# Four reorderings in a hybrid encoder block: scan products in three rows a chunk, the last convolution taps behind the gating, a block split behind a copy, part loads behind residual tiles

## The chip, the core and the metric

The kernel runs on one core of one Trainium2 chip. The core's engines run beside each other, each with a queue of its own that it works off in order: TensorE (PE in the profile) multiplies matrices, VectorE (DVE), ScalarE (ACT) and GpSimd (POOL) work elementwise, and SyncE (SP) issues the DMAs. Semaphores tie the queues together. The metric is the device time of one launch in microseconds; of several runs the median is taken.

## The reference

One layer over 1024 tokens of width 1024, everything in float32:

```python
h = rms_norm(x, mix_norm_g)
p = h @ w_in                                   # split into the inputs of three groups
y_a = spatial_gating(gelu(gm_u), gelu(gm_v))   # layer norm, causal 128x128 blocks, 4 heads
y_b = silu(layer_norm(depthwise_conv31(cv_a * sigmoid(cv_g)) + b))
y_c = gated_deltanet(dn_q, dn_k, dn_v, ...)    # chunked scan, 4 heads of 128
x = x + concat(y_a, y_b, y_c) @ w_out
h = rms_norm(x, ffn_norm_g)
x = x + (silu(h @ w_gate) * (h @ w_up)) @ w_down
return rms_norm(x, final_norm_g)
```

## The kernel before

Activations lie transposed, 128 features on the partitions by tokens; the 1024 tokens are two halves of 512 (`hf` 0 and 1). A float32 operand of a large product is split into a high part, cast on ACT (name ending in `_h`), and the remainder, subtracted on DVE (`_l`); each product of two operands is three matmuls, high by high, high by low, low by high. All matmuls of 128x512 go through PE in an order that a scheduling layer writes down while the kernel is built: it records all operations, models each engine as a queue and lets the first ready operation of the program's order go ahead, so a statement's place in the code, its data and explicit `tc.issue_after(...)` constraints decide where the instruction lands. Pools with few buffers (50 tiles `d`, 4 PSUM tiles `mm`, 3 `aux`, 2 raw weight buffers) make an operation wait for the one that frees its tile.

The stages around the change, in order of time:

- **Scan (245 to 350 us; lines 487 to 600).** The gated delta rule in 8 chunks of 128 tokens. `prep(c)` (L487) inverts a triangular matrix per head by blocks of 32 and 64: `pw` (L504) 8 products of 32x32, `pm` and `pmt` (L509, L515) 4 and 8 of 32x32, `pw2` (L519) and `pm2` (L524) 4 each of 64x64, with small copies on ACT and DVE between. The loop then does per chunk `ks` (L554, keys by state `Sn`), DVE's `vsr` (L556), `u` (L560), `S` (L567) with DVE's state `Sn` (L573), `os` (L580), `o` (L585), four 128x128 products each. Between them PE works on projection matmuls `pv` (L635) and `pg` (L258).
- **Gating and convolution.** `gating()` multiplies `sp` (L656) into `ugr` on DVE (L658). The depthwise convolution is 31 taps for each of 2 channel tiles `j` and 2 halves `hf`, all on DVE, 128x512 each (L692, L694): 120 instructions on L694.
- **Output projection (373 to 478 us; L757).** `mix_conv(0)` calls `conv_out(0)`: transposes `cvt` of the convolved first half (L704), statistics on DVE (L708, L709), normalization `ytk` on DVE (L714), transposes `cvb` back (L719), SiLU and a cast on ACT (`ybt`, then `myb_h`), the remainder on DVE (`myb_l`). Output tiles `po` of the first half are begun three at a time: 16 products each from `ya` and `yc`, then six from `myb`.
- **FFN (478 to 905 us).** Gate and up projections by a 7-product block scheme: blocks `B11`, `T1` to `T4`, `B22` of the activations, weights `w1` to `w7` of each `Matrix`. The products of a matrix accumulate in `X`; after the seventh, `product7` (L897), ACT copies `X` to `c22` (L900), and only then may PE add the fourth (`w4` by `T4`, L909). The block `T4` is made by subtractions on DVE (L1012), casts on ACT and remainders on DVE (`T_h`, `T_l`).
- **Down projection (905 us to the end).** `Down` objects `d00` to `d16` (group, output tile), in two groups of inputs. Each adds its products to residual tiles that come from HBM: `acc` (L1060) loads a tile `xad` from `X1d`, `add` (L1072) adds the product on DVE, `put` stores it. `product7` of a `Down` loads two tiles and adds `X` to the first, and PE's next product into `X` waits for that. `Group.load` (L1120) fetches the blocks (`T1f1`, `T2f1`, `T4f1`, ... of group 1) from HBM, four 256 KB DMAs each; weights `d_r` come as 512 KB DMAs (L137). All loads and stores stand in SP's one queue.

Of the kernel before, what the change touches and what calls it, by code (L numbers as in the profile page):

```python
# [38 lines left out]
def tile_kernel(ctx: ExitStack, tc: tile.TileContext, xT, wt, wub, wv, wout, wg, wu, wd, wdl,  # L39
# [447 lines left out]
    def prep(c):  # L487
        hf, i = divmod(c, NH)
        cs = slice(i * P, (i + 1) * P)
        M, MT, lt = d3(f"M{c}"), d3(f"MT{c}"), d3(f"ltr{c}")  # L490
        nc.sync.dma_start(M, Md[:, c * NH:(c + 1) * NH])
        nc.sync.dma_start(lt, LTd[:, c * NH:(c + 1) * NH])
        qk, vs, kd = d3(f"qkr{c}"), d3(f"vsr{c}"), d3(f"kd{c}")
        nc.sync.dma_start(vs, VSd[c])
        nc.sync.dma_start(kd, KTd[c])
        prep.loaded.append(nc.sync.dma_start(qk, QKd[c]).ins)
        DVE.transpose(MT.rearrange("p a b -> p (a b)"), M.rearrange("p a b -> p (a b)"))

        lo, up = (slice(0, 32), slice(64, 96)), (slice(32, 64), slice(96, 128))
        pw = aux3(f"pw{c}")  # L500
        for h in range(NH):
            for j, k in zip(lo, up):
                PE.matmul(pw[k, h, 0:32], lhsT=lt[j, h, k], rhs=M[j, h, j], start=True, stop=True)
        W = sp.tile([P, NH, 64], F32, tag="W", name="W")[:, :, 0:32]  # L504
        for k in up:
            ACT.copy(W[k], pw[k, :, 0:32])
        pm = aux3(f"pm{c}")
# [4 lines left out]
        for h in range(NH):
            for j, k in zip(lo, up):
                PE.matmul(pm[j, h, 0:32], lhsT=W[k, h], rhs=MT[k, h, k], start=True, stop=True)
        for j, k in zip(lo, up):  # L515
            DVE.tensor_scalar(MT[j, :, k], pm[j, :, 0:32], -1.0, None, op0=ALU.mult)
        pw = aux3(f"pw2{c}")
# [890 lines left out]
```

## Time and profile before

| | us |
|---|---|
| Median of three runs (1148.93 to 1153.93) | 1151.78 |
| The profiled execution | 1150.55 |
| Its span, first to last instruction | 1148.8 |
| PE busy in it | 1130.3 |
| DVE, ACT, POOL busy | 798.0, 479.1, 225.5 |
| Longest wait of PE for one operation | 3.0 |

PE works for 98% of the span; what the other engines do costs time only where PE stands still for it, or where the clock that is granted to it falls.

### The profile page before, as it was taken

The page shows a single profiled execution, that of the slowest core. Times are in us where ns is not written, and L with a number is a line of the kernel's source. Part 1 is how long each engine was busy: PE and PEld are TensorE (multiplying, and loading weights), DVE is VectorE, ACT ScalarE, POOL GpSimd, SP SyncE. Part 2 cuts the span into 40 slices and gives each one's busy share as a digit, 9 for nine tenths or more (in the row PEclk, how much of TensorE's full clock was granted, in tenths as well). Part 3 has the DMA queues.
Part 4 walks back from the last instruction along what each step waited for, and adds up shares of the span by engine and source line. Part 5 has one row for each costly group of instructions (what it writes and reads, how often), then busy time and mean ns, then how long its engine had stood idle before and what let it go on. Part 6 is the DMA issues. An engine that isn't in the chain of part 4 may idle for free.

```text
span 1148.8 us, 15996 instructions
## 1 busy us (share of the span) xinstructions
PE 1130.3 (98%) x5878; PEld 934.7 (81%) x5878; DVE 798.0 (69%) x1297; ACT 479.1 (42%) x1006; POOL 225.5 (20%) x192
## 2 busy tenths in 40 slices
PE   9999999999999999989999999999999999899997
PEld 7889888889788888877888888888888877688897
DVE  6799879868889757696654655565544786685623
ACT  7456561224435654453333333333334533432522
POOL 0000230011213221205432323323232000000142
PEclk9999999999999999999999999999999999999999
DMA  7134342463423454314332322232234778778312
GB/s 241 57 118 167 111 138 102 123 208 112 131 65 109 147 182 167 129 37 140 136 110 83 129 92 101 92 129 92 100 129 151 247 243 280 249 266 277 146 70 78
DMA packets 87325, 163.17 MB, mean 142 GB/s; under 512 B 16432, under 2 KB 28368, under 8 KB 87248
## 3 DMA queue, kind: packets, MB, share of 16 engines
q1 hardware_dynamic: 87248, 162.16, 42.0%
q8 instruction: 46, 0.75, 0.3%
q14 instruction: 31, 0.25, 0.1%
HBM read 115.45 MB, written 46.68 MB: 141 GB/s over the span
## 4 chain that ended last, share of the span: by engine, by line
PE 66%; DVE 4%; DMA 2%; issue 1%; SPq 0%; POOL 0%; ACT 0%; POOLq 0%; ACTq 0%; DVEq 0%
PE Xu L836 10%; PE Xg L836 10%; PE po L757 8%; PE Xd L836 7%; PE pdl L1158 5%; PE Zu L836 5%; PE Zg L836 5%; PE pg L258 3%; PE Zd L836 3%; PE Yu L836 2%; PE Yg L836 2%; PE Yd L836 2%; DMA d_r<-in_wd_dram 1%; PE Wu L836 0%; DVE T_l L90 0%
## 5 line engine op out<-in xcount | busy, mean ns | idle before, releaser
L694 DVE SCALAR_TENSOR_TENSOR ca<-cy,vec,ca 128x512 f32<-128x512 f32 x120 | 92.6, 794 | 0.5
L1342 POOL TENSOR_TENSOR sqf<-sqf,sqt 128x256 f32<-128x256 f32 (+1 forms) x19 | 17.9, 940 | 228.3 <-ACT sqt L1340 228.1
L131 DVE TENSOR_TENSOR wo_l<-wo_r,wo_h 128x512 fp32r<-128x512 f32 x32 | 26.6, 843 | 20.0 <-ACT wo_h L130 20.0
L901 DVE TENSOR_TENSOR c22u<-Zu,c22u 128x512 f32<-128x512 f32 x11 | 7.6, 692 | 45.0 <-ACT c22u L900 45.0
L1074 DVE TENSOR_TENSOR xad<-Xd,xad 128x512 f32<-128x512 f32 x32 | 21.8, 688 | 24.1 <-PE Xd L836 14.2
L885 POOL TENSOR_TENSOR s2u<-u_r,s2u 128x512 f32<-128x512 f32 x11 | 19.7, 1787 | 85.8 <-DVE w6u_l L131 85.8
L819 POOL TENSOR_TENSOR sqa<-sqa,xr 128x512 f32<-128x512 f32 x13 | 17.7, 1362 | 71.1 <-ACT xr L817 45.2
L1158 PE MATMUL pdl<-ff_h,wd_h 128*128 128x256 f32 (+1 forms) x96 | 30.9, 322 | 0.0
L1158 PE MATMUL pdl<-ff_h,wd_l 128*128 128x256 f32 (+1 forms) x96 | 30.6, 319 | 0.0
L1158 PE MATMUL pdl<-ff_l,wd_h 128*128 128x256 f32 (+1 forms) x96 | 30.5, 318 | 0.0
L885 POOL TENSOR_TENSOR s2g<-g_r,s2g 128x512 f32<-128x512 f32 x11 | 18.1, 1642 | 62.6 <-DVE w6g_l L131 62.6
L870 POOL TENSOR_TENSOR s1g<-g_r 128x512 f32<-128x512 f32 x11 | 14.2, 1293 | 76.3 <-DMA g_r<-in_wg_dram 76.3
L836 PE MATMUL Yu<-b,w2u_h 128*128 128x512 f32 x88 | 27.9, 396 | 0.0
L836 PE MATMUL Xu<-b,w1u_h 128*128 128x512 f32 x88 | 27.6, 395 | 0.0
L836 PE MATMUL Xg<-b,w1g_h 128*128 128x512 f32 x88 | 27.5, 394 | 0.0
L836 PE MATMUL Yg<-b,w2g_h 128*128 128x512 f32 x88 | 27.5, 393 | 0.0
L1333 DVE TENSOR_TENSOR xf<-pdl,xf 128x256 f32<-128x256 f32 (+1 forms) x18 | 9.2, 514 | 25.9 <-PE pdl L1158 25.8
L130 ACT CAST wo_h<-wo_r 128x512 fp32r<-128x512 f32 x32 | 19.6, 618 | 18.0 <-PE po L757 14.7
L870 POOL TENSOR_TENSOR s1u<-u_r 128x512 f32<-128x512 f32 x10 | 14.6, 1455 | 62.3 <-DMA u_r<-in_wu_dram 57.2
L131 DVE TENSOR_TENSOR w2g_l<-g_r,w2g_h 128x512 fp32r<-128x512 f32 x11 | 16.2, 1476 | 15.0 <-ACT w2g_h L130 15.0
L900 ACT COPY c22u<-Xu 128x512 f32<-128x512 f32 x11 | 6.5, 587 | 47.8 <-PE Xu L836 47.8
L900 ACT COPY c22g<-Xg 128x512 f32<-128x512 f32 x11 | 6.4, 586 | 46.8 <-PE Xg L836 46.8
(580 smaller groups left out, 3869.9 us busy)
## 6 DMA issues: line engine op xcount, KB each, us to landing
u_r<-in_wu_dram SPq DMA_DIRECT2D x24, 512.0 KB, 3.9
g_r<-in_wg_dram SPq DMA_DIRECT2D x24, 512.0 KB, 3.8
d_r<-in_wd_dram SPq DMA_DIRECT2D x24, 512.0 KB, 5.0
wo_r<-in_wout_dram SPq DMA_DIRECT2D x16, 512.0 KB, 4.1
xad<-X1d SPq DMA_DIRECT2D x32, 256.0 KB, 5.0
X1d<-xad SPq DMA_DIRECT2D x28, 256.0 KB, 3.3
FFd<-T SPq DMA_DIRECT2D x24, 256.0 KB, 2.0
xr<-in_xT_dram SPq DMA_DIRECT2D x16, 256.0 KB, 3.7
```

The source lines that it names most:

```text
L130: ACT.copy(hi, raw)
L131: DVE.tensor_tensor(lo, raw, f32(hi), op=ALU.subtract)
L258: proj.last = PE.matmul(ps[hf], lhsT=cols(wtile, a, kt * P), rhs=(xh, xl)[b][kt][hf], start=(kt == 0 and a + b == 0), stop=(kt == KT - 1 a ...
L694: DVE.scalar_tensor_tensor(o, y(m), w(m), o, op0=ALU.mult, op1=ALU.add)
L757: out_mm.last = PE.matmul(ps, lhsT=cols(wtile, a, kt * P), rhs=mix[hf][kt][b], start=(kt == 0 and a + b == 0), stop=(kt == 3 and a == 1))
L819: POOL.tensor_tensor(acc, acc, xr, op=ALU.add)
L836: ins = PE.matmul(ps, lhsT=w[a][:, k * P:(k + 1) * P], rhs=blk[b][k], start=(first and k == 0 and a + b == 0), stop=(last and k == HB - 1 ...
L870: eng.tensor_tensor(self.s1, a21, a22, op=ALU.add)
L885: (eng or POOL).tensor_tensor(self.s2, self.part(0, 1), self.s2, op=ALU.subtract)
L1074: self.added = DVE.tensor_tensor(x, ps, x, op=ALU.add).ins
L1158: PE.matmul(ps[:, 0:cs.stop - cs.start], lhsT=cols(wtile, a, c), rhs=ff[f, hf][b][:, cs], start=(first and i + a + b == 0), stop=(last and ...
L1342: POOL.tensor_tensor(acc[:, 0:w], acc[:, 0:w], t[:, 0:w], op=ALU.add)
```

## The change

1. `prep` becomes a class `Prep` with four steps. `pm` and `pmt` write one PSUM tile and stand together (`small2`); the loop calls the steps so that small products of the coming chunk stand in a row behind `ks`, before `u` and behind it, and `issue_after` ties them so: `ks` and `large2` in one row, `u` and `small2` in one row, `large1`, `S` in one row. Head 3 goes first in `ks` and `u`.
2. The 30 L694 taps of `j` = 1, `hf` = 1 may be issued on DVE only behind the last instruction of `gating()`.
3. The first of the four T4 subtractions and its cast come before the copy of `c22`; the other three casts come behind the copy, and the addition to `c22` and the two to `c12` behind the remainders. On ACT the activation to `c21g`, which reads `X` after the T4 products, now stands before the cast `w6u_h` instead of behind it; on DVE the order from the last remainder to `w6u_l` (addition to `c22g`, `s1u`, `c12g`, `s2u`, `s3u`, `c12g`, `w6u_l`) is what it was.
4. In the down part `T4` of a group and `T2`, `T1` of the next group are loaded behind the residual loads of `product7` (`m.accs`), no longer ahead of them.

```diff
+    now = Prep(0)
+    for step in (now.small1, now.small2, now.large1, now.large2):
+        step()
     for c in range(NC):
+
         hf, i = divmod(c, NH)
         cs = slice(i * P, (i + 1) * P)
-        MT, qk, vs, kd = ready
-        if c < NC - 1:
-            ready = prep(c + 1)
+        MT, qk, vs, kd = now.MT, now.qk, now.vs, now.kd
+        nxt = Prep(c + 1) if c < NC - 1 else None
+        last = None
         if c > 0:
             pk = aux3(f"ks{c}")
-            for h in range(NH):
-                PE.matmul(pk[:, h], lhsT=kh[hf][:, h, cs], rhs=S[:, h], start=True, stop=True)
+
+            for h in (3, 0, 1, 2):
+                with behind(last):
+                    last = PE.matmul(pk[:, h], lhsT=kh[hf][:, h, cs], rhs=S[:, h], start=True, stop=True).ins
+            last = now.large2(last)
             for h in range(NH):
                 DVE.scalar_tensor_tensor(vs[:, h], pk[:, h], neg[:, c, h:h + 1], vs[:, h],
                                          op0=ALU.mult, op1=ALU.add)
+        if nxt:
+            nxt.small1(last)
         pu = aux3(f"u{c}")
-        for h in range(NH):
-            PE.matmul(pu[:, h], lhsT=MT[:, h], rhs=vs[:, h], start=True, stop=True)
+        last = None
+        for h in (3, 0, 1, 2):
+            with behind(last):
+                last = PE.matmul(pu[:, h], lhsT=MT[:, h], rhs=vs[:, h], start=True, stop=True).ins
         u = d3(f"u{c}")
         DVE.tensor_tensor(u, pu, bk[:, c].unsqueeze(2).to_broadcast([P, NH, P]), op=ALU.mult)
         So = S
         if c < NC - 1:
+            nxt.small2(last)
+            last = nxt.large1()
             pS = aux3(f"S{c}")
-            for h in range(NH):
-                PE.matmul(pS[:, h], lhsT=kd[:, h], rhs=u[:, h], start=True, stop=True)
+            with behind(last):
+                for h in range(NH):
+                    PE.matmul(pS[:, h], lhsT=kd[:, h], rhs=u[:, h], start=True, stop=True)
             S = d3(f"Sn{c}")
...
             for hf in range(2):
-                DVE.scalar_tensor_tensor(ug[hf][:, :, cs], ps[:, hf * NH:(hf + 1) * NH],
-                                         vec[:, V_BS + h:V_BS + h + 1], ug[hf][:, :, cs],
-                                         op0=ALU.add, op1=ALU.mult)
+                gating.last = DVE.scalar_tensor_tensor(ug[hf][:, :, cs], ps[:, hf * NH:(hf + 1) * NH],
+                                                       vec[:, V_BS + h:V_BS + h + 1], ug[hf][:, :, cs],
+                                                       op0=ALU.add, op1=ALU.mult).ins
...
             DVE.tensor_scalar(o, y(0), w(0), vec[:, V_DWB + j:V_DWB + j + 1], op0=ALU.mult, op1=ALU.add)
             for m in range(1, 31):
-                DVE.scalar_tensor_tensor(o, y(m), w(m), o, op0=ALU.mult, op1=ALU.add)
+
+                with tc.issue_after(gating.last) if j * hf else ExitStack():
+                    DVE.scalar_tensor_tensor(o, y(m), w(m), o, op0=ALU.mult, op1=ALU.add)
...
-        def product7(self):
+        def product7(self, behind=None):
+
             product(self.X, self.w7, self.blk["T3"], False, False)
             self.c22 = dt(f"c22{self.name}")
             self.freed = ACT.copy(self.c22, self.X).ins
-            DVE.tensor_tensor(self.c22, self.Z, self.c22, op=ALU.add)
+            self.parted = None
+            if behind:
+                self.freed, self.parted = behind(self.freed)
+            with tc.issue_after(self.parted) if self.parted else ExitStack():
+                DVE.tensor_tensor(self.c22, self.Z, self.c22, op=ALU.add)
...
     behind_t3 = split_b.last
+
+    def sub_t4(k):
+        DVE.tensor_tensor(b0[HB + k], b0[HB + k], b0[k], op=ALU.subtract)
+
+    T4[0][0], T4[1][0] = (dt(f"T40{i}", F32R) for i in range(2))
     with tc.issue_after(behind_t3):
         m.weight4()
+        sub_t4(0)
+        cast = ACT.copy(T4[0][0], b0[HB]).ins
+
+    def parts_t4(freed):
+
+        ins = behind_t3
         for k in range(HB):
-            DVE.tensor_tensor(b0[HB + k], b0[HB + k], b0[k], op=ALU.subtract)
-            split_d(T4, k, b0[HB + k], "T4")
+            with tc.issue_after(ins):
+                if k < HB - 1:
+                    sub_t4(k + 1)
+                if k:
+                    with tc.issue_after(freed):
+                        split_d(T4, k, b0[HB + k], "T4")
+                    last, ins = split.last
+                else:
+                    ins = DVE.tensor_tensor(T4[1][0], b0[HB], f32(T4[0][0]), op=ALU.subtract).ins
+        return last, ins
+
+    with tc.issue_after(product.last), tc.issue_after(cast):
+        m.product7(parts_t4)
...
         new, coming = opener.get(i + 1), opener.get(i + 3)
-        if coming and i - 1 not in opener:
+        if coming and i <= FT:
             coming.load("T2", "T1")
         if new:
-            new.load("B11", "B21", "T4")
+            new.load("B11", "B21")
...
-        m.product7()
+        if i > 0:
+            m.product7()
+        with tc.issue_after(m.accs) if isinstance(m, Down) else ExitStack():
+            if new:
+                new.load("T4")
+            if opener.get(i + 2) and i > FT:
+                opener[i + 2].load("T2", "T1")
...
                 with tc.issue_after(nxt.loaded):
                     for dst, t in late:
                         nc.sync.dma_start(dst, t)
-                    if coming:
-                        coming.load("T2", "T1")
                 late = []
```

Two places in the queues. DVE in the output projection, from the gate of the last head (`sg`) towards the normalization `ytk` of the first half: before

```order
L675 TENSOR_TENSOR sg_3727<-pg_0_3652,rbc_372 128x512
L675 TENSOR_TENSOR sg_2719<-pg_1_3653,rbc_373 128x512
L708 BN_STATS st<-ytk_3891 128x6 x2
L709 BN_AGGR mvc<-st 128x2
L131 TENSOR_TENSOR wo_l<-wo_r,wo_h 128x512
L709 BN_AGGR mvc<-st 128x2
L708 BN_STATS st<-ytk_3891 128x6 x2
L90 TENSOR_TENSOR myc_l<-yc_2694,myc_h 128x512
L709 BN_AGGR mvc<-st 128x2 x2
L711 RECIPROCAL cr<-sdc 128x4
L714 TENSOR_SCALAR ytk_3891<-ytk_3891,mvc,cr 128x256 x4
```

and now, as far as the same point of the statistics; L735 is the tap line, L749 and L750 the statistics:

```order
L735 SCALAR_TENSOR_TENSOR ca_3729<-cy_3086,vec,ca_3729 128x512 x5
L714 TENSOR_TENSOR sg_3719<-pg_0_3644,rbc_372 128x512
L714 TENSOR_TENSOR sg_2706<-pg_1_3645,rbc_373 128x512
L735 SCALAR_TENSOR_TENSOR ca_3729<-cy_3086,vec,ca_3729 128x512
L749 BN_STATS st<-ytk_3883 128x6
L735 SCALAR_TENSOR_TENSOR ca_3729<-cy_3086,vec,ca_3729 128x512
L750 BN_AGGR mvc<-st 128x2
L749 BN_STATS st<-ytk_3883 128x6
L735 SCALAR_TENSOR_TENSOR ca_3729<-cy_3086,vec,ca_3729 128x512
L89 TENSOR_TENSOR myc_l<-yc_2681,myc_h 128x512
L735 SCALAR_TENSOR_TENSOR ca_3729<-cy_3086,vec,ca_3729 128x512
L750 BN_AGGR mvc<-st 128x2
```

All 30 taps of `j` = 1, `hf` = 1 now stand between the last `ugr` (row 454) and `ytk` (row 496); before, 12 of them stood behind the last `ugr` and none behind `sg`.

SP's queue in the down part, before (`xad0601`, `xad0611` and `xad0610` are the residual tiles of `Down` d06, `d120` and `d121` weights of d12):

```order
L1129 DMA T4f1l0_8732<-FFd_5123 128x512
L1129 DMA T4f1l1_8733<-FFd_5123 128x512
L1070 DMA X1d_3862<-xad0401_8575 128x512
L1129 DMA T4f1l2_8734<-FFd_5123 128x512
L1129 DMA T4f1l3_8735<-FFd_5123 128x512
L1062 DMA xad0601_8740<-X1d_3862 128x512
L1062 DMA xad0611_8784<-X1d_3862 128x512
L1062 DMA xad0610_8786<-X1d_3862 128x512
L137 DMA d120_r_8803<-in_wd_dram 128x1024
L137 DMA d121_r_8805<-in_wd_dram 128x1024
```

and now:

```order
L1131 DMA xad0601_8724<-X1d_3854 128x512
L1139 DMA X1d_3854<-xad0401_8551 128x512
L1131 DMA xad0611_8768<-X1d_3854 128x512
L1131 DMA xad0610_8770<-X1d_3854 128x512
L1198 DMA T4f1l0_8787<-FFd_5130 128x512
L1198 DMA T4f1l1_8788<-FFd_5130 128x512
L1198 DMA T4f1l2_8789<-FFd_5130 128x512
L1198 DMA T4f1l3_8790<-FFd_5130 128x512
L136 DMA d120_r_8795<-in_wd_dram 128x1024
L136 DMA d121_r_8797<-in_wd_dram 128x1024
```

The four T4f1 loads and the three residual loads have changed places, with one store between. In the same way `xad0401`, `xad0411` and `xad0410` have moved ahead of the eight loads of T2f1 and T1f1; the weights `d060`, `d061` behind them stand where they stood.

## Rows read from the trace of the kernel before

**Rows 1.** The page, busy time of each engine: time, share of the span, instructions.

```profile
PE 1130.3 (98%) x5878; PEld 934.7 (81%) x5878; DVE 798.0 (69%) x1297; ACT 479.1 (42%) x1006; POOL 225.5 (20%) x192
```

**Rows 2.** Waits of PE: who waited for whom, total us, times, longest.

```profile
PE Xd L836 <- DVE xad L1074: 4.5, 3, 3.0
PE Xg L836 <- ACT c22g L900: 2.9, 1, 2.9
```

**Rows 3.** Timeline of PE in the scan: start, length (us), engine, line, operation, tiles.

```profile
245.81 0.28 PE L635 MATMUL pv<-wv_h,xh 128*128 128x256 f32 x1
246.02 0.67 PE L519 MATMUL pw<-M,ltr 64*64 64x64 f32 x8
246.62 0.39 PE L635 MATMUL pv<-wv_h,xl 128*128 128x256 f32 x1
```

**Rows 4.** Timeline of DVE, from the gating to the convolution's output.

```profile
349.76 0.88 DVE L658 SCALAR_TENSOR_TENSOR ugr<-sp,vec,ugr 128x256 f32<-128x256 f32 x2 [0.19 <-PE sp L656]
351.32 2.32 DVE L694 SCALAR_TENSOR_TENSOR ca<-cy,vec,ca 128x512 f32<-128x512 f32 x3
356.62 3.60 DVE L694 SCALAR_TENSOR_TENSOR ca<-cy,vec,ca 128x512 f32<-128x512 f32 x3
378.95 1.39 DVE L714 TENSOR_SCALAR ytk<-ytk,mvc,cr 128x256 f32<-128x256 f32 x4
```

**Rows 5.** Timeline of POOL beside it.

```profile
356.78 5.79 POOL L600 TENSOR_TENSOR q<-q,pack 128x512 f32<-128x512 f32 x4 [20.62 <-DVE pack L597]
```

**Rows 6.** Busy time of the engines from 351.3 to 380.4, then of line 694.

```profile
351.30:380.40 29.10, 29.10 (x148) 23.51 (x147) 26.57 (x42) 18.73 (x37) 14.78 (x10) 1.00 0.35 118
351.30:380.40 29.10, 11.03 (x12) 1.00 0.35 118
```

**Rows 7.** Timeline of PE in the output projection.

```profile
372.84 0.60 PE L704 MATMUL cvt<-ident,ca 128*128 128x128 f32 x4
373.20 0.47 PE L757 MATMUL po<-mya_h,wo_h 128*128 128x512 f32 x1
379.53 0.29 PE L719 MATMUL cvb<-ident,ytk 128*128 128x128 f32 x1
385.98 0.39 PE L757 MATMUL po<-myb_h,wo_h 128*128 128x512 f32 x1
```

**Rows 8.** Timeline of ACT in the output projection.

```profile
382.90 0.62 ACT L89 CAST myb_h<-ybt 128x512 fp32r<-128x512 f32 x1
```

**Rows 9.** Timeline of PE where the block T4 begins.

```profile
512.54 0.80 PE L836 MATMUL Xg<-T_h,w4g_h 128*128 128x512 f32 x1 [2.89 <-ACT c22g L900]
516.76 0.39 PE L836 MATMUL Xu<-T_h,w6u_h 128*128 128x512 f32 x1
```

**Rows 10.** Timeline of ACT where the block T4 begins.

```profile
515.59 0.62 ACT L130 CAST w6u_h<-s2u 128x512 fp32r<-128x512 f32 x1 [0.64 <-DVE s2u L871]
```

**Rows 11.** Timeline of DVE where the block T4 begins.

```profile
513.07 0.69 DVE L901 TENSOR_TENSOR c22g<-Zg,c22g 128x512 f32<-128x512 f32 x1
516.67 0.69 DVE L131 TENSOR_TENSOR w6u_l<-s2u,w6u_h 128x512 fp32r<-128x512 f32 x1
```

**Rows 12.** Busy time of the engines, two microseconds in the down part.

```profile
980.00:982.00 2.00, 1.80 (x4) 1.49 (x5) 0.06 (x1) 0.00 (x0) 0.00 (x0) 0.50 0.94 378
```

**Rows 13.** Timeline of PE in the down part.

```profile
956.86 0.47 PE L836 MATMUL Xd<-T3hT3f,w7d_h 128*128 128x512 f32 x1 [1.16 <-DVE xad L1074]
980.20 0.77 PE L836 MATMUL Xd<-T3hT3f,w7d_h 128*128 128x512 f32 x1 [2.99 <-DVE xad L1074]
985.33 0.50 PE L836 MATMUL Xd<-T4f0h,w4d_h 128*128 128x512 f32 x1 [0.32 <-DVE xad L1074]
```

**Rows 14.** Timeline of ACT in the down part.

```profile
959.35 0.62 ACT L130 CAST w1d_h<-d_r 128x512 fp32r<-128x512 f32 x1 [10.34 <-DMA d_r<-in_wd_dram]
982.70 0.62 ACT L130 CAST w1d_h<-d_r 128x512 fp32r<-128x512 f32 x1 [7.78 <-PE Xd L836]
```

**Rows 15.** Timeline of SP's queue in the down part.

```profile
975.97 0.90 SPq L137 DMA_DIRECT2D d_r<-in_wd_dram  x2
```

More of the change, by code (lines that the diff above doesn't have):

```diff
@@ L88, in split @@
         hi, lo = dt(f"{name}_h", F32R), dt(f"{name}_l", F32R)
-        ACT.copy(hi, src)
-        DVE.tensor_tensor(lo, src, f32(hi), op=ALU.subtract)
+        split.last = ACT.copy(hi, src).ins, DVE.tensor_tensor(lo, src, f32(hi), op=ALU.subtract).ins
         return hi, lo
@@ L484, in tile_kernel @@
             nc.sync.dma_start(VSd[hf * NH:(hf + 1) * NH, :, h].rearrange("c p v -> p c v"), t)
[L487 to L500, printed above, removed]
-        for h in range(NH):
-            for j, k in zip(lo, up):
[L503 to L507, printed above, removed]
-        for h in range(NH):
-            PE.matmul(pm[32:64, h, 0:32], lhsT=MT[32:64, h, 32:64], rhs=W[32:64, h], start=True, stop=True)
-        DVE.tensor_scalar(M[32:64, :, 0:32], pm[32:64, :, 0:32], -1.0, None, op0=ALU.mult)
-        pm = aux3(f"pmt{c}")
-        for h in range(NH):
[L513 to L517, printed above, removed]
-        for h in range(NH):
-            PE.matmul(pw[64:128, h, 0:64], lhsT=lt[0:64, h, 64:128], rhs=M[0:64, h, 0:64], start=True, stop=True)
-        W2 = sp.tile([P, NH, 64], F32, tag="W", name="W2")
-        ACT.copy(W2[64:128], pw[64:128, :, 0:64])
-        pm = aux3(f"pm2{c}")
-        for h in range(NH):
-            PE.matmul(pm[0:64, h, 0:64], lhsT=W2[64:128, h], rhs=MT[64:128, h, 64:128], start=True, stop=True)
-        DVE.tensor_scalar(MT[0:64, :, 64:128], pm[0:64, :, 0:64], -1.0, None, op0=ALU.mult)
-        POOL.tensor_tensor(kd, kd, ekd[:, c].unsqueeze(2).to_broadcast([P, NH, P]), op=ALU.mult)
-        return MT, qk, vs, kd
@@ L543, in tile_kernel @@
     S = None
-    ready = prep(0)
+    now = Prep(0)
+    for step in (now.small1, now.small2, now.large1, now.large2):
+        step()
     for c in range(NC):
@@ L600, in tile_kernel @@
                 POOL.tensor_tensor(o, o, rr[:, hf * NH + i2].unsqueeze(2).to_broadcast([P, NH, P]), op=ALU.mult)
+        now = nxt
         if c == NH:
@@ L797, in tile_kernel @@
             pss = [mm_ps(f"po{hf}{m}") for m in ns]
-            wts = [load_w(wout[m], f"wo{hf}{m}", prep.loaded[min(6 + m, 7)] if hf == 0 and n == 0 else None) for m in ns]
+            wts = [load_w(wout[m], f"wo{hf}{m}", prep_loaded[min(6 + m, 7)] if hf == 0 and n == 0 else None) for m in ns]
             for ps, m, wtile in zip(pss, ns, wts):
@@ L913, in end4 @@
             product(self.X, self.w4, self.blk["T4"], False, True)
-            for ps in (self.Z, self.W):
-                DVE.tensor_tensor(self.c12, ps, self.c12, op=ALU.add)
+            with tc.issue_after(self.parted) if self.parted else ExitStack():
+                for ps in (self.Z, self.W):
+                    DVE.tensor_tensor(self.c12, ps, self.c12, op=ALU.add)
     ffn = {"B11": B11, "B21": B21}
```

65 lines of the change are left out of this document (60 added, 5 removed).

## Prediction

> **What bounds the kernel now.** I read the shares of busy time first, then the list of PE's waits, then, stage by stage, the timelines of the engine that PE waits for. PE is busy for 1130.3 us of a span of 1148.8 [rows 1], so all its idle time together is 18.5 us, and no reordering can win more than that plus what a lowered clock costs. The reader should see in the list of waits that only two entries are worth more than a microsecond and are aimed at here: 4.5 us for residual tiles of the down projection and 2.9 us for the copy of `c22g` [rows 2]. They name who came last, not what comes next. So at each place I ask what PE needs after the wait, and when that is ready.
>
> **Part 1, the scan: -0.3 us.** A row of eight small products among projection matmuls runs from 246.02 to 246.62, 0.60 us, and 0.21 us pass from the projection matmul at 245.81 to its start [rows 3], while a plain 256-column step, estimated as half a 512-column one of 0.24 (below), is 0.12: entering costs about 0.09. A chunk has five such rows before and three now, most of them next to 128x128 products instead of projection matmuls. Two entries less in seven chunks, 2 x 7 x 0.09 = 1.3 us, is the upper gain. The lower bound is a loss of 1.5 us: `ks` now follows `o` with nothing between to cover DVE's `Sn`, some 0.2 us in each of seven chunks. I take -0.3, nearer to the row's price than to the guess about the wait.
>
> **Part 2, the taps: +6.2 us.** This looks free, since the 30 moved taps are not needed until the second half. But DVE works in order, and in the new order all 30 stand between the last `ugr` and `ytk`, the normalization of the first half, which PE needs for `cvb` and then `myb`.
>
> Before: the last `ugr` starts at 349.76 and `ytk` ends at 378.95 + 1.39 = 380.34 [rows 4]. From 351.3 on DVE is busy for 26.57 of 29.10 us, 11.03 of it with 12 taps, so 15.5 us with other instructions; only 2.5 us are free [rows 6]. Where does the new stretch begin? In the new order 80 `pg` matmuls and 32 transposes stand between the last `sp` and the first `cvt`. The transposes take (373.20 - 372.84) / 4 = 0.09 each; from 373.20 to 385.98 PE does 48 products and 12 transposes without a gap, so a product takes (12.78 - 1.1) / 48 = 0.24 [rows 7]. Counted back from 372.84, less the 0.3 of part 1: 372.5 - 19.2 - 2.9 = 350.4, and with two `ugr` of 0.88 together [rows 4] 351.3; in a run of one kind a matmul takes a little less than that mean, so I take 351.9.
>
> A tap takes 2.32 / 3 = 0.77 in a run and 3.60 / 3 = 1.20 beside the first instructions of POOL's L600 [rows 4, 5], which now end before the taps. I take 0.72, since a tap followed by another operation overlaps with its end. Of the 15.5 us two small instructions of the scan's end, 0.3, now come earlier. `ytk` then ends at 351.9 + 15.2 + 30 x 0.72 = 388.7, 8.3 us later than before.
>
> PE meets `cvb` behind 44 products in the new order: 372.5 + 8 x 0.09 + 44 x 0.24 = 383.8. The first of the four `ytk` instructions ends 1.04 before the last, at 387.6: a wait of 3.8 us. From the end of `ytk` to a ready `myb_h` it was 382.90 + 0.62 - 380.34 = 3.2 us [rows 8], and the cast of a weight now stands between, 0.5: 392.4. PE gets there with 9 products and 8 transposes after the first `ytk`, the last `cvb` at 388.8, so at about 391.3: 1.1 us more. `myb_l` follows in the shadow of the products by `myb_h`. After the idle stretch of 2.99 us before 980.20 the granted clock is 0.50 for the two microseconds shown [rows 12, 13]; at half rate these lose 1.0, and with the way back up I take 1.3 here. Sum 3.8 + 1.1 + 1.3 = 6.2. Bounds: with taps of 0.65 and the others 2.2 shorter, 13.0, `ytk` ends at 384.4 and the cost is zero; with taps at the stretch's mean, 11.03 / 12 = 0.92 [rows 6], it ends at 394.7 and the cost is 12.2. A gain is excluded, PE having no gap there before.
>
> A rule weighed: POOL worked 14.78 us in that stretch [rows 6], and taps beside it took 1.20 instead of 0.77 [rows 4, 5]. In the Trainium skill ("SBUF — State Buffer", section "SBUF: two separate sides") a GpSimd instruction and a DVE instruction with two SBUF inputs exclude each other for a whole instruction. The trace shows about half of that loss. By the rule in full, the 14.78 - 5.79 = 9.0 us of POOL's work that remain beside the taps would all be lost to DVE, and `ytk` would end at 388.7 + 9.0 = 397.7 at most.
>
> **Part 3, T4: 0.** With three casts out of its way the copy can start when `w7` is through, at 512.54 - 2.89 = 509.65, and with 0.6 for the copy `w4` by T4 begins at about 510.3 [rows 9]. Its 12 products would end at 513.1; the last remainders of T4, which DVE finishes by 513.07 [rows 11], hold it until about 513.9. But the next products need `w6u_h`, cast at 515.59 [rows 10], and `w6u_l`, which DVE makes at 516.67 as the seventh in an unbroken row from 513.07 [rows 11]. DVE's instructions up to there are as many as before and in the same order, so PE arrives at 513.9 and waits until 515.59 + 0.62 = 516.2, where before it began at 516.76 [rows 9]. That is -0.5 with full clock and +0.8 if the clock falls in the new gap; the best that could be had is the whole wait and its half clock, -4.5. I take 0: the wait moves from ACT's copy to DVE's chain.
>
> **Part 4, the down part: -2.6 us.** Two waits go. The first, 1.16 us before 956.86 [rows 13], opens the way to `w1d`, whose cast starts at 959.35, released by the DMA of its weights [rows 14]. Ahead of these weights SP issues the same loads and stores as before, in another order, among them a store that waits for DVE in both; so they land when they did, and `w1d` is ready at 960.0. Before, PE was through with `w7` at 956.86 + 12 x 0.24 = 959.7 and hardly waited; now it is through at 958.5 and stands the 1.2 us there. I count 0.3 for small waits behind it. The second, 2.99 us before 980.20, with half clock behind it and 0.32 us at 985.33 [rows 13], ends because `xad0601` is issued four loads earlier. But d12's weights, issued at 975.97 [rows 15] behind the same bytes, are cast at 982.70 [rows 14]. PE would be through with `w7` at 980.20 - 2.99 - 0.3 + 2.8 = 979.7, then, after 0.9 for the addition of `X`, with the seven products of `w4` that come next at 982.3, and stands until 982.70 + 0.62 = 983.3. Before, it had done two products of `w1` and none of `w4` at 985.33 [rows 13], so as many as now at 985.33 + 5 x 0.24 = 986.5: 3.2 gained. Of that I let 0.9 be given back at the weights of d14, which wait for a buffer that d12's free. Sum -0.3 - 3.2 + 0.9 = -2.6. Bounds: -7 if nothing else comes last, +1 if the T2f1 and T1f1 loads, now issued just ahead of `d060`, delay it.
>
> **Sum.** -0.3 + 6.2 + 0 - 2.6 = +3.3: 1150.55 + 3.3 = 1153.9 for the profiled execution, whose time lies 1.2 below the median of the runs; with the median it is 1155.1. I predict 1154.5.
>
> **Rivals.** (A) The forecast, a wait at `cvb` of 2 to 6 us and a gain of 2 to 3 in the down part: 1151 to 1158. (B) DVE absorbs the taps, as it does if they run at 0.65 and the others are shorter without POOL's L600: 1151.8 - 2.9 = 1149. For it speaks that the new order has 44 products ahead of `cvb` where there were 30, as if its writer's model saw no wait behind them; against it that DVE had 2.5 us free and gets 18 taps more. (C) All named waits go, no others come, and the taps are free: -0.3 - 4.5 - 7 = -11.8, 1140; against it stand the chains of parts 3 and 4. (D) The slower end: taps and POOL hinder each other in full, taps at 0.92 or more, so that `ytk` ends at 394.7: 12.2 - 2.9 = +9.3, 1161. It decides from `ytk` ending after about 391.3, where the loss passes 5.8 net (391.3 - 388.7 + 3.3 = 5.9). For it speaks the mean of [rows 6]; against it that 4 of its 12 taps ran beside L600. The rule of "SBUF — State Buffer" in the Trainium skill would lead to this case or beyond it.
>
> **Chances.** A 0.55, B 0.15, C 0.08, D 0.22. Runs of this kernel differ by 0.4%, so 0.5%, 5.8 us, is what a measurement can tell. Faster than 1146 is C and a fifth of B, 0.11; slower than 1157.5 is D and a tenth of A, 0.27; the rest is 0.62. The range for 8 in 10 leaves out C and half of D: 1147 to 1161. A alone: 1151 to 1158.
>
> **What would show it.** Taps at DVE from 352 to 388 without a gap, PE idle before `cvb` near 384 with a lowered clock behind it: part 2. PE idle at 514 to 516 with `w6u_h` as the releaser: part 3. PE waiting for `w1d_h` and no longer for `xad` at 958 and 982: part 4. The forecast is wrong if PE has no gap at `cvb`, or if the gap before T4 is gone without another.

## The result: 1.3% slower

The changed kernel takes 1165.75 us in the median of four runs (1161.61 to 1169.91), the kernel before 1150.95 beside it: ratio 1.0126, 95% interval 1.0103 to 1.0149. I had 1154.5 with a range of 1147 to 1161, so the time lies outside it. The profiled execution took 1161.61 with a span of 1159.7, 10.9 more than before; the other three were slower at a mean granted clock of 0.987 to 0.992 instead of 0.995, and what they lost beyond the profiled one is not located.

Where the 10.9 us came in is read from the starts of the same PE instruction in both traces: the first `pw`, the first `cvt`, the first `Xu` by `w1u_h`, the first `Wg` by `w3g`, the first `Xd` by `w1d_h`, the first `pdl`. The differences of the stretches between them, in us against the kernel before, for the profiles of all runs (the time ahead of the first `pw` is left out):

```
                    scan   out.proj.  FFN start  T4, FFN   down    end
predicted           -0.3     +6.2        -         0.0     -2.6     -
after               -1.1     +8.6      +0.1       +1.9     +1.1   +0.3
e1  part 2 alone    -0.1    +12.2      +0.1       +0.4     +1.1   +0.2
e4  part 1 alone    +5.6      0.0       0.0        0.0     +0.4    0.0
e5  10 taps free    +0.8     +3.3       0.0       +1.5     +4.4   +0.4
e6  no part 2       +3.0      0.0       0.0       -0.1     +3.5   +0.4
e9  taps late       -0.5     +8.3       0.0       -0.6     -0.9   +0.2
e12 taps after ytk  -0.5    +11.3      +4.7       +0.3     -1.9   +0.5
e2  part 3 alone     0.0      0.0       0.0       +1.5     -0.4   +0.6
e7  sums on POOL    +0.2      0.0       0.0       +1.8     +0.8    0.0
e11 sums earlier    +0.2      0.0       0.0       -1.2     -0.6    0.0
e3  part 4 alone     0.0      0.0       0.0        0.0     +0.7   +0.4
e8  B22 held        +0.2      0.0       0.0        0.0     +5.6   +0.3
e10 part 4 mended   -0.2      0.0       0.0        0.0     -2.3   +0.8
e13 3+4 mended      +0.1      0.0       0.0       -1.2     -3.9   +0.5
e14 all mended      -1.0    +11.7      +4.6       -1.7     -3.5   +0.6
```

Each row is one execution, and stretches that a run does not edit differ too: T4 and the FFN by -0.6 to +0.4 (e9, e1), the down part by -1.9 to +1.1 (e12, e1). So the +1.1 of the down part tells nothing by itself. The four profiles with part 4 as it is (after, e5, e6, e3) have 2.4 there in the mean, the three with part 4 mended (e10, e13, e14) -3.2, the seven without it -0.2.

PE is busy for 2.4 us more than before [rows 1]; the rest of the 10.9 is new idle time. Line of busy time after:

```profile
PE 1132.7 (98%) x5878; PEld 936.1 (81%) x5878; DVE 794.0 (68%) x1297; ACT 478.8 (41%) x1006; POOL 222.9 (19%) x192
```

PE's waits after, to be held against [rows 2] (total, times, longest): `c22g` has gone from 2.9 to 0.7 and `xad` has stayed, but four others have come.

```profile
PE Xd L877 <- DVE xad L1143: 5.0, 3, 2.4
PE po L798 <- DVE wo_l L130: 4.0, 1, 4.0
PE Xu L877 <- ACT w6u_h L129: 2.3, 1, 2.3
PE Xd L877 <- ACT w1d_h L129: 2.0, 2, 1.5
PE cvb L760 <- DVE ytk L755: 1.9, 1, 1.9
```

The taps, DVE in the changed kernel (start, duration, idle time before in brackets): the answer to [rows 4]. The last `ugr` starts at 349.87, the 30 taps end at 387.9, and `ytk` ends at 389.19; I had 388.7. What the constraint takes from DVE lies ahead of that: in 334 to 350 us DVE is now busy for 6.1 of 16 us, before for 13.9.

```profile
349.87 0.88 DVE L697 SCALAR_TENSOR_TENSOR ugr<-sp,vec,ugr 128x256 f32<-128x256 f32 x2 [1.22 <-PE sp L695]
...
385.00 0.65 DVE L130 TENSOR_TENSOR wo_l<-wo_r,wo_h 128x512 fp32r<-128x512 f32 x1
...
387.14 0.75 DVE L735 SCALAR_TENSOR_TENSOR ca<-cy,vec,ca 128x512 f32<-128x512 f32 x1
387.81 1.38 DVE L755 TENSOR_SCALAR ytk<-ytk,mvc,cr 128x256 f32<-128x256 f32 x4
...
419.90 1.38 DVE L755 TENSOR_SCALAR ytk<-ytk,mvc,cr 128x256 f32<-128x256 f32 x4
```

PE in the same place, where [rows 7] had no gap. It stops at 381.71, two microseconds ahead of where I had put the stop (383.8, at `cvb`), for a weight remainder that stands in DVE's row between the last taps (385.00 above); `cvb` then needs no wait. A second stop comes at the `cvb` of the second half.

```profile
385.71 0.51 PE L798 MATMUL po<-myc_h,wo_l 128*128 128x512 f32 x1 [4.00 <-DVE wo_l L130]
388.37 0.45 PE L760 MATMUL cvb<-ident,ytk 128*128 128x128 f32 x1
392.18 0.66 PE L760 MATMUL cvb<-ident,ytk 128*128 128x128 f32 x4 [0.34 <-ACT ybt L762]
420.46 0.56 PE L760 MATMUL cvb<-ident,ytk 128*128 128x128 f32 x2 [1.90 <-DVE ytk L755]
```

Behind the first stop the granted clock (the last column but two) is near 0.50, that is 1.2 instead of 2.4 GHz: 2 x 0.48 + 2 x 0.37 = 1.7 us lost.

```profile
384.00:386.00 2.00, 0.29 (x1) 1.00 0.00 0
386.00:388.00 2.00, 2.00 (x6) 0.52 0.39 135
388.00:390.00 2.00, 1.99 (x8) 0.63 0.66 258
```

The second stop has another cause than a full DVE, which stands idle for 10.2 us between the two `ytk`. SP issues the load of a residual tile `xr` at 413.41 (before at 404.90, while PE is 5.6 later here), DVE waits 2.28 us for it, ACT waits for DVE's sum, and ACT's copy of the transposed second half, which feeds the statistics and `ytk`, stands behind that in ACT's queue. The load is late by a chain that goes back to DVE's row of remainders of the second half, which starts 9.3 us later than before (403.07 and 393.80). The first line is from the kernel before:

```profile
404.90 0.33 SPq L810 DMA_DIRECT2D xr<-in_xT_dram  x1
```

```profile
413.41 0.33 SPq L851 DMA_DIRECT2D xr<-in_xT_dram  x1
416.21 0.69 DVE L852 TENSOR_TENSOR x<-po,xr 128x512 f32<-128x512 f32 x1 [2.28 <-DMA xr<-in_xT_dram]
416.98 0.63 ACT L858 ACTIVATE xr<-x 128x512 f32<-128x512 f32 x1 [1.97 <-DVE x L852]
417.52 0.57 ACT L746 COPY ytk<-cvt 128x512 f32<-128x512 f32 x1
```

T4, PE after, against [rows 9]: the wait is where I put it, at `w6u_h`.

```profile
517.96 0.73 PE L877 MATMUL Xg<-T,w4g_h 128*128 128x512 f32 x2 [0.67 <-ACT c22g L942]
520.44 0.50 PE L877 MATMUL Xg<-T_l,w4g_h 128*128 128x512 f32 x1 [0.24 <-DVE T_l L89]
524.32 0.51 PE L877 MATMUL Xu<-T_h,w6u_h 128*128 128x512 f32 x1 [2.32 <-ACT w6u_h L129]
```

The down part, PE after, against [rows 13]. The two waits ahead of `w7` in d04 and d12 have gone, and `w1d_h` stands in for the first with 1.46 (I had 1.2); for the second there are 0.88 and 0.53 (I had 1.0 at `w1d_h`). New are the first and the last row, ahead of `w7` in d00 and d10, the opening tiles of the two groups.

```profile
937.93 0.47 PE L877 MATMUL Xd<-T3hT3f,w7d_h 128*128 128x512 f32 x1 [1.73 <-DVE xad L1143]
970.23 0.73 PE L877 MATMUL Xd<-B11f,w1d_h 128*128 128x512 f32 x2 [1.46 <-ACT w1d_h L129]
990.89 0.47 PE L877 MATMUL Xd<-T4f0h,w4d_h 128*128 128x512 f32 x1 [0.88 <-DVE xad L1143]
993.29 0.73 PE L877 MATMUL Xd<-B11f,w1d_h 128*128 128x512 f32 x2 [0.53 <-ACT w1d_h L129]
1022.22 0.47 PE L877 MATMUL Xd<-T3hT3f,w7d_h 128*128 128x512 f32 x1 [2.42 <-DVE xad L1143]
```

### The profile page after: what moved, and what is told of

It reads as the page before. It is cut to its first block, busy times and chain, and to the rows that moved or that the text cites. A ratio compares the mean times of both kernels' runs of the same rounds, so it can differ in the third digit from the quotient of the medians.

```text
span 1159.7 us, 16003 instructions
## 1 busy us (share of the span) xinstructions
PE 1132.7 (98%) x5878; PEld 936.1 (81%) x5878; DVE 794.0 (68%) x1297; ACT 478.8 (41%) x1006; POOL 222.9 (19%) x192
## 4 chain that ended last, share of the span: by engine, by line
PE 81%; DVE 9%; DMA 6%; issue 2%; SPq 1%; ACT 1%; POOL 0%; POOLq 0%; ACTq 0%; DVEq 0%
PE Xu L877 10%; PE Xg L877 9%; PE pdl L1227 5%; PE po L798 5%; PE Zg L877 4%; PE Zu L877 4%; PE Xd L877 4%; PE pv L257 4%; PE pq L257 4%; PE pg L257 3%; PE pk L257 3%; PE pk L205 3%; PE Zd L877 2%; DMA d_r<-in_wd_dram 2%; PE pv L674 2%
## 5 line engine op out<-in xcount | busy, mean ns | idle before, releaser
L735 DVE SCALAR_TENSOR_TENSOR ca<-cy,vec,ca 128x512 f32<-128x512 f32 x120 | 92.3, 787 | 0.8
L798 PE MATMUL po<-myc_h,wo_l 128*128 128x512 f32 x64 | 26.1, 407 | 4.0 <-DVE wo_l L130 4.0
L798 PE MATMUL po<-myc_h,wo_h 128*128 128x512 f32 x64 | 26.0, 406 | 0.0
L798 PE MATMUL po<-myc_l,wo_h 128*128 128x512 f32 x64 | 25.9, 405 | 0.0
```

The lines of the kernel that those rows point to most:

```text
L735: DVE.scalar_tensor_tensor(o, y(m), w(m), o, op0=ALU.mult, op1=ALU.add)
L798: out_mm.last = PE.matmul(ps, lhsT=cols(wtile, a, kt * P), rhs=mix[hf][kt][b], start=(kt == 0 and a + b == 0), stop=(kt == 3 and a == 1))
```

## The experiments

**Each part alone.** The edits are the four parts of the diff, one at a time on the kernel before.

> The kernel before with part 2 alone (30 taps behind the gating). Theory P, the losses of the profile after belong to the parts in which they stand and add up: the output projection took 8.6 us longer there, so this kernel takes 1150.9 + 8.6 = 1159.5, with PE idle 3 to 5 us around 385 to 389 (weight remainder wo_l and cvb) and about 2 us at the second half's cvb near 420. Theory I, the parts need each other (the other orders of DVE and SP set up the waits): the taps alone cost the 6.2 us that I forecast or less, 1157 at most, without a wait at the second cvb.

> The kernel before with part 1 alone (small products in three rows). Theory P: -1.0 us, 1149.9, all of it between the first pw and the first cvt. Theory I: nothing, 1150.9; the 1.1 us that the profile after shows there come from the taps that no longer stand between DVE's operations of the scan.

Measured: part 2 alone 1164.76 (ratio 1.0118, 1.0097 to 1.0139), part 1 alone 1156.62 (1.0051, 1.0026 to 1.0076). Both theories missed the size. Alone, part 2 costs 12.2 in the output projection, with the stops that theory P named (6.3 us at `wo_l`, 2.1 at the second `cvb`), and part 1 costs 5.6 in the scan; together they cost 7.5. By the medians part 2 alone is as slow as all four parts (1.0118 and 1.0126), and the four ratios of the single parts would add up to 2.1%: the parts do not add. In part 1 alone DVE starts a row of 13 taps just ahead of what the gating needs, PE waits for `ugr`, and the mean granted clock is 0.93 in 334 to 350 and 0.90 in 350 to 372. Its DVE:

```profile
334.26 12.09 DVE L734 SCALAR_TENSOR_TENSOR ca<-cy,vec,ca 128x512 f32<-128x512 f32 x13
...
347.47 0.87 DVE L698 SCALAR_TENSOR_TENSOR ugr<-sp,vec,ugr 128x256 f32<-128x256 f32 x2
```

and its PE:

```profile
348.39 1.22 PE L696 MATMUL sp<-vg,wsm 128*128 128x256 f32 x2 [2.93 <-DVE ugr L698]
```

The reason lies further ahead. In 300 to 334 us DVE does 19 taps before, 11 in part 1 alone and 10 in the changed kernel (busy time of the tile `ca` in these stretches). It has no more idle time there (busy for 31.7, 30.1 and 30.3 of 34 us); with part 1 other instructions take the place, 59 and 58 instead of 41, the gating's normalization `vg` among them. Part 1 alone leaves more of the convolution to the time from 334 on.

> The changed kernel without part 2 (taps as before). Theory J, parts 1 and 2 belong together: part 1 alone lets 13 taps start at DVE ahead of what the gating needs and PE waits 2.9 us for ugr, with a lowered clock behind it (5.6 us up to the first cvt); so this kernel has that wait and 1150.9 + 5.6 + 1.7 + 1.0 = 1159. Theory P, part 1 wins 1.1 wherever the taps stand: 1165.75 - 8.6 = 1157 or, with the 12.1 us that part 2 costs by itself, 1153.6, without a wait for ugr.

```diff
-                with tc.issue_after(gating.last) if j * hf else ExitStack():
-                    DVE.scalar_tensor_tensor(o, y(m), w(m), o, op0=ALU.mult, op1=ALU.add)
+                DVE.scalar_tensor_tensor(o, y(m), w(m), o, op0=ALU.mult, op1=ALU.add)
```

1158.62 (1.0063, 1.0040 to 1.0086), with 2.9 us for `ugr`: theory J, though the granted clock stayed at 1.00 behind that wait in this profile, so that the stretch cost 3.0 instead of 5.6. That J's 1159 came out is luck: by the profile its terms 5.6, 1.7 and 1.0 (scan, T4, down) are 3.0, -0.1 and 3.5. What part 1 wins in the scan, it loses again unless the taps step aside.

**Where should the taps go?** First ten of them free (`and m > 10` in the condition of part 2):

> The changed kernel, but only the last 20 of the 30 taps wait for the gating; the first 10 may go earlier. Theory Q, the loss at the output projection is the place of the taps in DVE's queue: in the changed kernel DVE stands still for 2.95 and 4.42 us between 333.9 and 342.3, room for about 9 taps of 0.92; with 10 taps there the normalization ytk ends about 10 x 0.75 = 7.5 us earlier, near 382, the waits of 4.0 at wo_l and 1.9 at the second cvb go, and no wait of PE for ugr comes: 1165.75 - 8.6 = 1157. Theory R, taps cost there because POOL works beside them: the 20 that stay still run at 1.4 to 1.8 us beside POOL and ytk is late all the same, 1161 to 1164.

1160.64 (1.0077, 1.0051 to 1.0103), between the two. The output projection costs 3.3 instead of 8.6, `ytk` starts at 382.95 instead of 387.81, but 0.8 us for `ugr` and 3.1 for `cvb` remain, and the taps beside POOL's L638 take 9.09 us for 8, 1.14 each. The down part of this profile is 3.3 us slower than that of the changed kernel, which no part of the edit explains.

Then the 30 taps recorded last (and so with the lowest precedence), first still behind the gating. In this run they read the tokens of the first half instead of the second; the instructions are the same in number and shape.

```diff
+    def late_taps():
+        with tc.issue_after(gating.last):
+            ...
             if n == 6 and hf == 0:
+                late_taps()
                 mix_conv(1)
```

> The kernel before with parts 1 and 2, but the 30 taps, still behind the gating, are written down only ahead of the second half's normalization, so that everything the first half needs goes before them at DVE. Theory Q, the loss is the place of the taps ahead of the wo_l remainders and of ytk: no wait at wo_l or at the first cvb, ytk of the first half at or before 380; the 20 us of taps fill DVE's idle time up to 410, of which there were 8 us in 372 to 392 and 7 more up to 420, so a wait of at most 3 us comes at the second half's cvt or cvb; with the 1.1 us of part 1 the total is 1150 to 1154, against 1158 for parts 1 and 2 as they are. Theory V, DVE simply has too much to do from 334 on (10 taps more than before are left there with part 1), wherever the taps stand: what is saved at the first half comes back in full at the second, 1157 to 1160.

1158.02 (1.0055, 1.0042 to 1.0068), with 5.5 us at the first `cvb`: 26 of the taps still stood ahead of `ytk`; why the scheduling layer put them there is not shown. That tells nothing on the question, so the taps were tied to `ytk` itself (`tc.issue_after(conv_out.last)`, the last `ytk` of the first half):

> The kernel before with parts 1 and 2, but the 30 taps wait for the first half's ytk instead of the gating. Theory Q, the loss of part 2 is the place of the taps ahead of the first half's remainders and ytk: no wait of PE up to the first myb, the first cvb about 6.7 us behind the first cvt as before. DVE had 8.2 us idle in 372 to 392, 1.1 in 392 to 400 and 2.2 in 400 to 410, 11.5 together, and gets 20 us of taps, so the second half's cvt comes 4 to 8 us late, of which its 18 us of products of other inputs cover a part: total 1150 to 1156. Theory V, DVE has too much to do behind 334 and every place of the taps costs the same: PE waits 5 us or more for the second half and the total is 1157 to 1160, as with the taps behind the gating.

1165.15 (1.0124, 1.0106 to 1.0142): theory V in kind, but 5 us beyond its time. The first half is as clean as Q wanted, `cvb` 6.69 us behind `cvt` as before, but DVE has lost the time up to there and the second half is late. Behind that, PE waits 2.8 us at the start of the FFN for sums of squares (`ssx`) that POOL and ACT prepare. DVE of this run, with the idle time ahead of each row, 14.0 us in four of them:

```profile
353.32 0.69 DVE L131 TENSOR_TENSOR wo_l<-wo_r,wo_h 128x512 fp32r<-128x512 f32 x1 [1.94 <-ACT wo_h L130]
358.22 0.69 DVE L90 TENSOR_TENSOR mya_l<-ya,mya_h 128x512 fp32r<-128x512 f32 x1 [4.21 <-ACT mya_h L89]
363.30 0.69 DVE L90 TENSOR_TENSOR mya_l<-ya,mya_h 128x512 fp32r<-128x512 f32 x1 [1.80 <-ACT mya_h L89]
372.44 1.29 DVE L715 TENSOR_TENSOR sg<-pg,rbc 128x512 f32<-128x512 f32 x2 [6.04 <-PE pg L258]
```

and its PE:

```profile
411.13 0.50 PE L805 MATMUL po<-myc_h,wo_l 128*128 128x512 f32 x1 [1.16 <-DVE wo_l L131]
425.06 0.90 PE L751 MATMUL cvt<-ident,ca 128*128 128x128 f32 x3 [4.42 <-DVE ca L740]
```

So the cost is the time in which DVE may not do the taps: the kernel before does 18 of the 30 ahead of the last `ugr`; with part 1 other instructions stand there up to 334, and where DVE then has room the constraint forbids them. Beside the new scan every place tried costs 3 us or more up to the FFN; the least is e6, where they stand as before.

**T4.**

> The kernel before with part 3 alone (T4 split behind the copy of c22). Theory P: +2.0 to +2.6 us, 1153 to 1153.5; the 2.9 us wait for c22g becomes 0.7, and 2.3 us stand at w6u_h instead, with a granted clock of 0.50 behind it for about 3 us. Theory I: the loss comes from the state in which the taps left the stage; alone the edit is worth 0, 1150.9, as forecast.

1152.77 (1.0016, 1.0001 to 1.0031): theory P in its waits and clock, a little under its time. PE starts `w6u_h` at 517.58, which is 0.1 earlier than before when both are counted from the first `pw`, so the edit moves a wait and wins nothing up to there. The 1.5 us come behind it. Granted clock in this run (PE busy, clock, DMA):

```profile
517.00:519.00 2.00, 1.42 (x5) 1.00 0.00 0
519.00:520.00 1.00, 1.00 (x4) 0.65 0.00 0
520.00:522.00 2.00, 2.00 (x6) 0.50 0.00 0
```

Before, the half clock lay at 512 to 516, behind the wait for `c22g` and ahead of `w6u_h`, which came at 516.2 only [rows 10]: most of what it took was time that PE would have stood still anyway. Now it lies behind the last wait, and all of it counts.

> The kernel before with part 3, and the three sums s1u, s2u, s3u of the next matrix on POOL instead of DVE. Theory C, the wait at w6u_h comes from DVE's row of seven instructions: POOL needs 1.5 + 1.8 = 3.3 us for s1u and s2u and can start behind the T3 parts, well before the row; w6u_h is ready when PE comes, the wait of 2.3 and the half clock behind it go, about 3.5 us less than part 3 alone, 1149. Theory R, POOL and DVE slow each other: the remainders T_l take 1.2 to 1.8 us instead of 0.69 and PE waits 2 us or more for T_l instead: 1152 or more.

```diff
-            m.sums(DVE if m is seq[1] or isinstance(m, Down) else POOL)
+            m.sums(DVE if isinstance(m, Down) else POOL)
```

1152.99 (1.0016, 1.0002 to 1.0030), nothing won: theory R, though its wait at `T_l` is 1.2 and not 2. The wait at `w6u_h` falls to 1.1, but beside POOL's sums two remainders take 2.38 (1.52 in part 3 alone), PE waits 1.2 for `T_l` and 0.5 for `w6u_l`, and the clock is at half in 518 to 521 all the same.

> The kernel before with part 3, and what the next matrix needs (sums s1u, s2u, s3u and casts of w6u) directly behind the remainders of T4, ahead of the additions to c22g and c12g on DVE and of the activations on ACT. Theory C2, PE waits for the chain s2u, w6u_h, and the half clock that follows the 2.3 us wait is what part 3 costs: w6u_h is ready 1.2 us earlier, the wait is 1.0 us, the clock stays at 1.00, and 2 us come back: 1150 to 1151, no more than 1 us off the kernel before. Theory R2, the granted clock falls all the same, since 1.7 us of short waits stand close together: 1152.5.

```diff
+        with tc.issue_after(ins):              # the last remainder of T4
+            seq[1].sums(DVE)
+            seq[1].weights65()
-        return last, ins                       # freed: the silus wait for it; parted: the additions
+        return split_w.first, seq[1].summed    # the cast of w6u; s3u
```

1150.07 (0.9989, 0.9977 to 1.0001): theory C2. `w6u_h` is cast at 514.82, PE waits 1.24 instead of 2.32, the clock stays at 1.00 up to 522, and the stage is 1.2 us shorter than before instead of 1.5 longer. Of these 2.6 us, 0.9 are the earlier start of `w6u_h` (both counted from the first `pw`) and 1.7 come behind it, where the waits are the same and only the clock differs. PE:

```profile
515.49 0.50 PE L835 MATMUL Xu<-T_h,w6u_h 128*128 128x512 f32 x1 [1.24 <-ACT w6u_h L129]
```

**The down part.**

> The kernel before with part 4 alone (loads of T4, T2, T1 behind the residual loads). Theory P: +1.4 us, 1152.3: the two waits for xad before w4 of d04 and d12 go or move to w1d_h, and two new ones stand where PE begins the tile of d00 (about 1.7 us) and of d10 (about 2.4 us), because the first residual tile of each opener is now issued behind the four B22 loads. Theory I: the new waits are only there because the stage began 10 us later against its DMA; alone the edit wins the 2.6 us that I forecast, 1148.3, with no wait for xad in d00 and d10.

1153.68 (1.0022, 1.0009 to 1.0034): theory P, the new waits are there (1.21 at d00, 2.57 at d10).

> The kernel before with part 4, and the B22 loads of a group held behind the first residual load of its opener (as they stood before). Theory S, the new waits of d00 and d10 come from the 1 MB of B22 loads that stands ahead of that residual tile in SP's queue: no wait for xad of over 0.5 us at the w7 product of d00 and d10, and 1.5 to 2.5 us less than part 4 alone, 1150 to 1151. Theory L, the tile is late because T4, T2 and T1 now share the DMA engines with it: the waits stay at 1.7 and 2.4 us and the time at 1152.5.

```diff
-            new.load("B22")
+                with tc.issue_after(m.accs):
+                    opener[i].load("B22")
```

1153.99 (1.0020, 1.0003 to 1.0038): theory S was wrong. d00 waits 1.70 as it did; at d10 the tile's wait falls to 1.43, but the weights behind B22 come late and 1.9 us stand at `w6d_h`. What I had missed is seen at SP of part 4 alone (issue, duration with the time that the queue stood):

```profile
885.69 10.43 SPq L137 DMA_DIRECT2D d_r<-in_wd_dram  x4
...
899.93 1.85 SPq L1129 DMA_DIRECT2D T4f0l<-FFd  x4
901.82 0.90 SPq L1062 DMA_DIRECT2D xad<-X1d  x2
```

Before, T4 of group 0 was issued at 885.58, right behind the B21 loads. Now it stands behind four weight loads that hold the queue for 10.4 us, 14 us later and directly ahead of the first residual tiles; the DMA engines are busy for 0.98 of 900 to 910 (0.83 before), and DVE stands 2.2 us for the first tile, after which it has a full row up to d00:

```profile
907.30 0.69 DVE L1074 TENSOR_TENSOR xad<-Xd,xad 128x512 f32<-128x512 f32 x1 [2.21 <-DMA xad<-X1d]
```

> The kernel before with part 4, except that T4 of group 0 is loaded where it was, ahead of the weights, and the B22 loads stand behind the weights of the opener's neighbour. Theory S2, the wait at d00 comes from T4 of group 0 being issued 14 us later, right ahead of the first residual tiles (DVE stands 2.2 us for the first of them, with the DMA engines at 0.98), and the one at d10 from B22 ahead of weights and tile: no wait of over 0.5 us at the w7 product of d00 and d10, the two waits at w1d_h and w4 of d12 stay near 1 us each, and the total is 1.5 to 2.5 us below part 4 alone, 1149.5. Theory L, the stretch is bound by the bytes: a wait of 1 to 3 us turns up at another tile or weight and the time stays at 1152 to 1153.

```diff
-            new.load("B11", "B21")
+            new.load("B11", "B21", *(() if isinstance(m, Down) else ("T4",)))
-            if new:
+            if new and isinstance(m, Down):
                 new.load("T4")
-            new.load("B22")
+                with tc.issue_after(nxt.loaded):
+                    opener[i].load("B22")
```

1148.58 (0.9982, 0.9973 to 0.9992), faster than before: theory S2, but for 1.03 us that stay at d10 and 2.0 instead of 1 at `w1d_h`. The wait at d00 is gone, and the stage is 2.3 us shorter; I had 2.6. PE's waits in the whole part:

```profile
958.88 0.73 PE L836 MATMUL Xd<-B11f,w1d_h 128*128 128x512 f32 x2 [2.01 <-ACT w1d_h L130]
979.55 0.47 PE L836 MATMUL Xd<-T4f0h,w4d_h 128*128 128x512 f32 x1 [0.88 <-DVE xad L1074]
1009.30 0.47 PE L836 MATMUL Xd<-T3hT3f,w7d_h 128*128 128x512 f32 x1 [1.03 <-DVE xad L1074]
```

**Together.**

> The kernel before with parts 3 and 4, both mended: the sums and the cast of w6u directly behind the remainders of T4; T4 of group 0 loaded where it was and B22 behind the weights. If the two gains add up (ratios 0.9989 and 0.9982 apart), 0.9971, 1147.7 us, with no wait over 0.3 us for w6u_l, c22g under 1 us, and none for xad over 1.1 us. If the earlier start of the down part meets transfers that are not there yet, 0.998 or more, 1149, with a wait at w1d_h or at xad of 2 to 3 us.

1148.95 (0.9985, 0.9975 to 0.9995), so faster than both kernels, but not faster than e10 by what these runs can tell. Its profile shows both gains, -1.2 and -3.9; its median does not show their sum.

> All four parts, with the taps behind the first half's ytk and parts 3 and 4 mended. If parts 1 and 2 with the taps there cost what they cost alone (theory Q: 0 to 5 us), the total is 1147 to 1152; if they cost 7 us (theory V), 1154 to 1156. Against 1165.75 of the changed kernel that is 11 to 18 us back, from where three kinds of instructions stand in their queues and with the same arithmetic.

1161.35 (1.0091, 1.0073 to 1.0108): worse than either case I gave, because parts 1 and 2 with the taps behind `ytk` cost 15 us here as in e12. Parts 3 and 4 keep their gains beside them (-1.7 and -3.5).

## Why the prediction was wrong

- **What bounds the kernel, and asking what comes next.** Right as a method: the waits for `c22g` and `xad` were replaced by the waits I named, `w6u_h` and `w1d_h`.
- **Part 1, -0.3.** The scan gained 1.1, within its bounds, but only beside part 2. Alone it is +5.6 (e4). I priced PE's rows and did not ask what DVE has to do when beside the new scan; the taps of part 2 were counted from 350 on only.
- **Part 2, +6.2.** The step "`ytk` then ends at 388.7" was hit (389.19) by luck, with errors that cancel: the last `ugr` ends at 350.7 instead of 351.3 and the taps follow at once where I had 351.9, the 30 taps took 25.8 us, 0.86 each instead of 0.72, and the rest of the stretch took some 12 instead of 15.2. The first half cost 6.6 (its sum said 6.2): 4.0 + 0.3 of idle time and 2.2 of longer busy time behind it, of which the two windows at a lowered clock show 1.7; it is `wo_l` that PE meets first. What failed is the sum's end: it stopped at `myb` of the first half and put the second at nothing. There 2.0 more were lost, 1.9 of them at `cvb`, by the late residual tile and not by a full DVE.
- **Rival D** (taps and POOL in each other's way, 1161) came nearest in size, by another cause. Its mark, `ytk` after 391.3, was not reached.
- **Part 3, 0.** "The wait moves from ACT's copy to DVE's chain" was right, and PE comes to `w6u_h` 0.1 us earlier than before (I had 0.5). Mis-sized is the clock: I gave it +0.8 as a bound and took 0, and it measured +1.5 alone and +1.9 in the changed kernel. The step that was missing: before, the half clock lay under a wait that was to come anyway. That it is the clock, e5 and e6 show: with the same waits the stretch cost +1.5 at half clock and -0.1 without.
- **Part 4, -2.6.** Failed is "SP issues the same loads and stores as before, in another order ... so they land when they did". I followed that for `w1d`, `xad04` and `xad06` and not for the openings of the groups. There T4 of group 0 came 14 us later, and B22 of group 1 ahead of a tile and weights; with T4 where it was and B22 behind the weights (e10) the part wins 2.3. d10 keeps 1.03 us, which stays open.
- **The sum.** +3.3 against +10.9 in the profile: +2.4 from part 2, +1.9 from part 3, +3.7 from part 4, -0.8 from part 1, and 0.4 in stretches that I had at nothing, makes 7.6. Parts 3 and 4 came out at or beyond the upper bounds that I had given them (+0.8 and +1). The shares by stretch are those of one profile and, for the down part, not surer than the spread given with the table. Another 4.1 us lie between the profiled execution and the median of 1165.75; no trace shows where.

## What to carry to other kernels

An instruction that is moved back on a busy engine is paid for by whoever reads that engine's next results, and then by all that is late behind them, on other engines and in the DMA queue: follow it to the last reader and not to the first, even across idle time of the engine. A constraint also leaves an engine idle where it had work; look for that time first. Where a load moves in a DMA queue, look at what the queue waits for at its new place and at what now stands behind it, in every repetition of the pattern. A lowered clock costs nothing while PE is ahead of its next wait; count it where no wait follows.
